# A conformer and sparse-attention decoder step: where the gate's loads land, and what the compressed branch and the cached rows queue behind

## The chip, the cores and the metric

The kernel runs on one core of one Trainium2 chip. The metric is the device time of one execution in microseconds (us); a comparison goes by the median of several executions. The core has five engines with an instruction queue each: PE (matrix products), DVE (vector), ACT (scalar activations and copies), POOL (a slower vector engine) and SP (which here only issues DMAs). A queue runs in order: an instruction that waits holds back all behind it on its engine.

## The reference

One inference step of a two-layer decoder, for a prompt of 512 tokens and 8 sequences of 4 new tokens each, 544 columns in all, width 1024. Only the first layer's first half and the cached keys matter here:

```
shift, scale, gate = split(silu(c) @ w_ada + b_ada)        # per sub-layer, width 3 x 1024
h = rmsnorm(x, g) * (1 + scale) + shift
u = h @ w_pw1 + b_pw1;  a, g = split(u);  u = a * sigmoid(g)
full = concat([state_conv, u])                             # 30 cached rows per decoded sequence
y = depthwise_conv(full, w_dw, 31 taps) + b_dw
x = x + gate * (silu(layernorm(y)) @ w_pw2 + b_pw2)
x = x + gate2 * swiglu(modulated rmsnorm(x))               # the first feed-forward layer
...
blk = cached pages, 32 rows a block, + pe_cmp              # compressed branch, of cached keys and values
cmp = silu(blk @ w_phi1 + b_phi1) @ w_phi2 + b_phi2        # used by the second layer's attention
```

The second layer is the attention (compressed, selected and window branches) and a second feed-forward layer.

## The kernel before

Activations stand with features on the 128 partitions: eight tiles f = 0 to 7 of 128 features, 544 columns each. A product in full precision is made of three products of split operands: each weight tile `raw` is split into `whi` (ACT, L169) and `wlo` (DVE, L170), the activations into `h_hi` and `h_lo`, and `products` (L176 to L186) issues, for each of eight k, three pairs of matmuls (L183, L185). So one product of 128 outputs is 48 matmuls, and each tile f of the convolution has two (gate and value).

**Order.** A scheduler puts each engine's instructions in an order ahead of time, by its own model of their durations, by program order and by priorities. `high_priority(-LATER)` marks a block as filler that goes into gaps. `issue_after(ins)` makes every instruction of its block that runs on the engine of `ins` stand behind `ins` in that engine's order; instructions of the block on other engines are bound only through their data.

**Buffers.** `raw` has four buffers of 512 KB. Every 512 KB load of weights goes into one of them, in the order of the program, and is issued on SP's queue, which stops until the buffer is free. `xt`, in the pool `shift`, has three buffers of just over two such slabs; the convolution uses them for shifted copies of its input (L714 to L724), the compressed branch for transposed cached rows.

**The stages that matter**, in order:

- *Modulation.* `ada_steps` (L446) makes one of scale, shift and gate: eight slabs of `w_ada`, each followed by four small matmuls (L452). `first_modulated` (L471) makes scale and shift of the first sub-layer; its generator `slabs` puts 12 of the 16 slabs two by two into `xt` and four into `raw`. The gate (`between` in `run`) uses `raw` alone, four slabs ahead of each tile f from f = 2 (`NSTEP`, L666).
- *Cached rows.* `state_parts` (L419) loads the cached convolution rows, transposes them on PE (16 transposes, L155), copies them on ACT (L431), multiplies them with the taps on POOL (16 multiplies, L439) and sums on DVE (16 reductions, L441). Its memory, the pool `setup`, then goes to the pool of the compressed branch.
- *Convolution.* `gated_units` (L645) makes `up` of each f (L677). Tiles 3 to 7 are convolved on PE as 64 matmuls of shifted copies (L730). Tiles 0 to 2 and half of tile 7 are convolved on DVE (`depthwise`, L734) as chains of 31 steps (L768), tile 7's chain last.
- *Layer norm and second product.* `layer_norm_out` (L798) sums over the features with PE (L812), subtracts the mean (L818), squares, takes the root and the reciprocal (L824), applies silu, splits, and multiplies with `w_pw2`; the residual follows.
- *Compressed branch.* `compress_steps` (L1032) takes the eight sequences one by one: two gathers of cached rows on POOL's DMA queue (`nat`, two buffers, L1030), four transposes on DVE (L1043), 32 matmuls of 128 columns on PE (L1049) and small work. For the first sequence it also makes a bias from `pe_cmp` (tile `hk`, DVE transpose L1025, 32 matmuls L1053, `bh` L1055). All 24 steps are issued as filler ahead of `depthwise`.
- *Feed-forward layer 0* follows, with what is left of the compressed branch, the bias tables, and the transposing and storing of all cached keys (`key_steps`, L1289) as its filler.

## Time and profile before

| what | value |
|---|---|
| time, median of 3 executions | 1660.17 us (1652.02 to 1661.15) |
| the profiled execution | 1661.26 us, span of its instructions 1659.5 us |
| PE busy | 1555.0 us, 94% of the span |
| DVE busy | 1107.8 us, 67% |
| ACT / POOL busy | 694.1 us, 42% / 235.2 us, 14% |
| moved by DMA | 295.26 MB, mean 178 GB/s |

A busy share is an average over stages that different engines limit. What a stage costs is read from the stretch of the profile where it lies: which engine is busy throughout, and which wait ends last. Times are counted from the span's start. In the profile each 32-bit matmul of these small products (L1049, L1053, L452, L812) shows as two passes, so its counts are double those of the program; the split products (L183, L185) show as one.

### The profile page before, as it was taken

The page shows a single profiled execution, that of the slowest core. Times are in us where ns is not written, and L with a number is a line of the kernel's source. Part 1 is how long each engine was busy: PE and PEld are TensorE (multiplying, and loading weights), DVE is VectorE, ACT ScalarE, POOL GpSimd, SP SyncE. Part 2 cuts the span into 40 slices and gives each one's busy share as a digit, 9 for nine tenths or more (in the row PEclk, how much of TensorE's full clock was granted, in tenths as well). Part 3 has the DMA queues.
Part 4 walks back from the last instruction along what each step waited for, and adds up shares of the span by engine and source line. Part 5 has one row for each costly group of instructions (what it writes and reads, how often), then busy time and mean ns, then how long its engine had stood idle before and what let it go on. Part 6 is the DMA issues. An engine that isn't in the chain of part 4 may idle for free.

```text
span 1659.5 us, 31626 instructions
## 1 busy us (share of the span) xinstructions
PE 1555.0 (94%) x12423; PEld 1366.8 (82%) x12423; DVE 1107.8 (67%) x2369; ACT 694.1 (42%) x1443; POOL 235.2 (14%) x270
## 2 busy tenths in 40 slices
PE   6897998999988889999999899999999999999997
PEld 3784677989978878999977677655699999999997
DVE  2897866482447788576657644867856865874865
ACT  5321115242222344255445422755746542552554
POOL 3444401021220112001110000000011110110010
PEclk9898979999999999999999999999999999999999
DMA  9577575374399999834779895746122472333231
GB/s 307 140 200 155 151 241 168 117 227 130 112 241 312 299 303 325 247 103 106 184 228 306 245 282 183 237 148 229 52 68 73 152 233 84 91 114 90 79 91 64
DMA packets 315568, 295.26 MB, mean 178 GB/s; under 512 B 16019, under 2 KB 275485, under 8 KB 311179
## 3 DMA queue, kind: packets, MB, share of 16 engines
q1 hardware_dynamic: 304507, 237.24, 48.7%
q0 software_dynamic: 10224, 55.47, 10.7%
q8 instruction: 98, 1.61, 0.4%
q10 hardware_dynamic: 688, 0.53, 0.1%
q14 instruction: 51, 0.42, 0.1%
HBM read 256.28 MB, written 45.48 MB: 182 GB/s over the span
## 4 chain that ended last, share of the span: by engine, by line
PE 65%; DMA 13%; DVE 10%; issue 6%; SPq 2%; ACT 2%; POOL 1%; ACTq 0%; DVEq 0%; POOLq 0%
PE g L185 18%; PE g L183 17%; PE g L247 8%; DMA raw<-in_w_down_dram 4%; PE t L247 3%; PE t L155 3%; PE o L1530 2%; DMA raw<-in_w_ada_dram 2%; DVE wlo L196 2%; PE t L1049 2%; PE a L452 1%; PE t L1379 1%; PE t L730 1%; PE sc L1509 1%; DVE y L768 1%
## 5 line engine op out<-in xcount | busy, mean ns | idle before, releaser
L169 ACT CAST whi<-raw 128x512 fp32r<-128x512 f32 x250 | 149.7, 606 | 408.7 <-PE g L185 280.1
L170 DVE TENSOR_TENSOR wlo<-raw,whi 128x512 fp32r<-128x512 f32 x250 | 173.0, 696 | 156.5 <-ACT whi L169 155.6
L183 PE MATMUL g<-h_hi,whi 128*128 128x256 f32 (+1 forms) x584 | 170.5, 293 | 13.9 <-DVE un L680 9.3
L185 PE MATMUL g<-h_hi,whi 128*128 128x288 f32 (+4 forms) x584 | 173.5, 298 | 0.9 <-ACT h_hi L575 0.9
L185 PE MATMUL g<-h_hi,wlo 128*128 128x288 f32 (+4 forms) x584 | 173.9, 298 | 0.0
L185 PE MATMUL g<-h_lo,whi 128*128 128x288 f32 (+4 forms) x584 | 173.7, 297 | 0.0
L183 PE MATMUL g<-h_lo,whi 128*128 128x256 f32 (+1 forms) x584 | 168.3, 288 | 3.0 <-DVE h_lo L830 3.0
L183 PE MATMUL g<-h_hi,wlo 128*128 128x256 f32 (+1 forms) x584 | 167.3, 287 | 0.0
L183 PEld LDWEIGHTS g<-h_hi,whi 128*128 128x128 f32 x584 | 111.5, 191 | 27.3 <-issue 16.2
L247 PE MATMUL g<-T,whi 128*128 128x272 f32 x656 | 127.9, 291 | 4.1 <-DVE sg L261 2.5
L195 ACT CAST whi<-s 128x512 fp32r<-128x512 f32 x128 | 79.1, 620 | 99.9 <-PE g L247 61.7
L183 PE MATMUL g<-a_hi,whi 128*128 128x256 f32 (+1 forms) x372 | 108.0, 291 | 12.4 <-ACT ht L912 4.3
L183 PEld LDWEIGHTS g<-h_lo,whi 128*128 128x128 f32 x584 | 111.8, 192 | 8.0 <-issue 4.3
L185 PEld LDWEIGHTS g<-h_hi,whi 128*128 128x128 f32 x584 | 111.3, 191 | 4.2 <-issue 2.9
L185 PEld LDWEIGHTS g<-h_hi,wlo 128*128 128x128 f32 x584 | 111.3, 191 | 2.6 <-issue 2.5
L185 PEld LDWEIGHTS g<-h_lo,whi 128*128 128x128 f32 x584 | 111.2, 190 | 2.6 <-issue 2.5
L183 PEld LDWEIGHTS g<-h_hi,wlo 128*128 128x128 f32 x584 | 111.5, 191 | 1.8 <-issue 1.7
L196 DVE TENSOR_TENSOR wlo<-s,whi 128x512 fp32r<-128x512 f32 x128 | 89.1, 698 | 34.0 <-ACT whi L195 32.2
L185 PE MATMUL g<-a_hi,wlo 128*128 128x288 f32 (+1 forms) x372 | 111.1, 299 | 0.0
L185 PE MATMUL g<-a_hi,whi 128*128 128x288 f32 (+1 forms) x372 | 110.9, 299 | 0.0
L185 PE MATMUL g<-a_lo,whi 128*128 128x288 f32 (+1 forms) x372 | 110.7, 298 | 0.0
L247 PEld LDWEIGHTS g<-T,whi 128*128 128x128 f32 x656 | 103.8, 190 | 5.6 <-ACT whi L195 2.2
(511 smaller groups left out, 4165.2 us busy)
## 6 DMA issues: line engine op xcount, KB each, us to landing
raw<-in_w_ada_dram SPq DMA_DIRECT2D x84, 512.0 KB
raw<-in_w_gate_dram SPq DMA_DIRECT2D x44, 512.0 KB
raw<-in_w_up_dram SPq DMA_DIRECT2D x44, 512.0 KB
raw<-in_w_down_dram SPq DMA_DIRECT2D x32, 512.0 KB
raw<-in_w_pw_dram SPq DMA_DIRECT2D x24, 512.0 KB
kt_d<-ktr SPq DMA_DIRECT2D x96, 128.0 KB
kt<-kt_d SPq DMA_DIRECT2D x24, 512.0 KB
raw<-in_w_kv_dram SPq DMA_DIRECT2D x20, 512.0 KB
```

The source lines that it names most:

```text
L155: self.te.transpose(out, in_, self.ident[:n, :n])
L169: self.s.copy(hi[:, :b - a], raw[:, a:b])
L170: self.v.tensor_tensor(out=lo[:, :b - a], in0=raw[:, a:b], in1=hi[:, :b - a].bitcast(F32), op=ALU.subtract)
L183: self.te.matmul(pg[:, 0, :split], a, b[:, i, :split], start=st, stop=sp)
L185: self.te.matmul(pg[:, 1, :tokens - split], a, b[:, i, split:tokens], start=st, stop=sp)
L195: self.s.copy(hi, src)
L196: self.v.tensor_tensor(out=lo, in0=src, in1=hi.bitcast(F32), op=ALU.subtract)
L247: self.te.matmul(out, a[:, i], b(i), start=first and i == 0 and j == 0, stop=i == 3 and j == 2, skip_group_check=not first)
L452: self.te.matmul(pa[32 * j:32 * j + 32, :256], self.cT[:, k, :], w[:, j * 256:(j + 1) * 256], start=k == 0, stop=k == KT - 1)
L730: self.te.matmul(pt[32 * gg:32 * gg + 32], wds[q // 4][:, gg, q % 4], vs[:, gg, 4 * q:4 * q + cols], start=q == 0, stop=q == 7)
L1049: te.matmul(ph[:, :P], self.w1[:, e, c // 2, c % 2], xv[:, c % 2, c // 2], start=c == 0, stop=c == 15)
L1530: te.matmul(po[rp * HD:(rp + 1) * HD, :256], self.vn[:, br, t, gg * HD:(gg + 1) * HD], pT[:, rp * 256:(rp + 1) * 256], start=br == 0 and t ...
```

## The change

Three edits. First, the generator of slabs becomes a method, `first_slabs`, that serves scale, shift and gate: 24 slabs, of which the last eight, the gate's, go into `xt` like most of those before, and none into `raw`. Second, the 24 steps of the compressed branch are issued after `depthwise` in the program, and inside `issue_after(self.last_step)`: their DVE instructions stand behind the last step of tile 7's chain. Third, the 16 transposes of the cached rows stand on PE behind the last matmul of the first tile's products (`first_product`).

```diff
--- before.py
+++ after.py
@@ -180,7 +180,7 @@
             whi, wlo = w[i]
             for j, (a, b) in enumerate([(whi, xhi), (whi, xlo), (wlo, xhi)]):
                 st, sp = i == 0 and j == 0, i == k - 1 and j == 2
-                self.te.matmul(pg[:, 0, :split], a, b[:, i, :split], start=st, stop=sp)
+                self.last_product = self.te.matmul(pg[:, 0, :split], a, b[:, i, :split], start=st, stop=sp).ins
                 if tokens > split:
                     self.te.matmul(pg[:, 1, :tokens - split], a, b[:, i, split:tokens], start=st, stop=sp)
         return pgs
@@ -427,7 +427,8 @@
             for f0 in range(0, KT, 4):
                 pt = self.bank()
                 for f in range(4):
-                    self.transpose(pt[:, f * 120:(f + 1) * 120], sc[:, a, (f0 + f) * P:(f0 + f + 1) * P])
+                    with self.tc.issue_after(self.first_product):
+                        self.transpose(pt[:, f * 120:(f + 1) * 120], sc[:, a, (f0 + f) * P:(f0 + f + 1) * P])
                 self.s.copy(us[:, f0:f0 + 4, a * 4:(a + 1) * 4, :CW - 1],
                             pt[:, :480].rearrange("p (f b w) -> p f b w", f=4, b=4))
         squares = sp.tile([P, D], F32, name="squares").rearrange("p (a n) -> p a n", a=2)[:, :, :4 * DS * (CW - 1)]
@@ -470,18 +471,7 @@
 
     def first_modulated(self, wsrc, rstd):
 
-        def slabs():
-            for i in range(2 * KT):
-                if 6 <= i < 10:
-                    yield self.wp.tile([P, KT, P], F32, name="raw", bufs=4).rearrange("p a b -> p (a b)")
-                else:
-
-                    if i % 2 == 0:
-                        two = self.shift_pool.tile([P, 4, SEQ + 28], F32, name="xt", bufs=3).rearrange("p a n -> p (a n)")
-                    yield two[:, i % 2 * D:(i % 2 + 1) * D]
-
-        made = slabs()
-        scale, shift = [self.ada_steps(0, part, b, lambda: next(made)) for part, b in ((1, "at"), (0, "bt"))]
+        scale, shift = [self.ada_steps(0, part, b, lambda: next(self.slabs)) for part, b in ((1, "at"), (0, "bt"))]
         for step in [scale] * KT + [shift] * 2:
             next(step)
         for _ in itertools.chain(scale, shift):
@@ -489,6 +479,17 @@
         ws = [self.weights(w) for w in wsrc]
         self.modulated(0, rstd)
         return ws
+
+    def first_slabs(self):
+
+        for i in range(3 * KT):
+            if 6 <= i < 10:
+                yield self.wp.tile([P, KT, P], F32, name="raw", bufs=4).rearrange("p a b -> p (a b)")
+            else:
+
+                if i % 2 == 0:
+                    two = self.shift_pool.tile([P, 4, SEQ + 28], F32, name="xt", bufs=3).rearrange("p a n -> p (a n)")
+                yield two[:, i % 2 * D:(i % 2 + 1) * D]
 
 
     def add_square(self, acc, src, f):
@@ -660,6 +661,7 @@
             cols = [wsrc[:, :, c * D + f * P:c * D + (f + 1) * P] for c in (1, 0)]
             if f == 0:
                 pg, pa = self.products(self.first_modulated(cols, self.rstd0), self.h_hi, self.h_lo, KT)
+                self.first_product = self.last_product
             else:
                 wg, wa = [self.weights(c) for c in cols]
                 for _ in range(NSTEP if f > 1 else 0):
@@ -765,8 +767,8 @@
                     if j == 0:
                         v.tensor_scalar(ps, x, w, self.b_dw[:, f:f + 1], op0=ALU.mult, op1=ALU.add)
                     else:
-                        v.scalar_tensor_tensor(out=ps, in0=x, scalar=w, in1=ps,
-                                               op0=ALU.mult, op1=ALU.add)
+                        self.last_step = v.scalar_tensor_tensor(out=ps, in0=x, scalar=w, in1=ps,
+                                               op0=ALU.mult, op1=ALU.add).ins
         for f in ORDER:
             finished(f, v)
         self.dump("y", y)
@@ -1674,7 +1676,8 @@
                 self.shift_pool = shifting.__enter__()
                 with sbuf("setup", "right") as sp:
                     self.setup(sp)
-                    between = self.ada_steps(0, 2)
+                    self.slabs = self.first_slabs()
+                    between = self.ada_steps(0, 2, slab=lambda: next(self.slabs))
                     ada1 = itertools.chain(*(self.ada_steps(1, part) for part in (1, 0, 2)))
                     units_ = self.gated_units(pool, between)
                     next(units_)
@@ -1684,13 +1687,13 @@
                 next(units_)
                 compress = self.compress_steps(self.compress_pool)
 
+                acc = self.depthwise(pool)
                 with tc.high_priority(-LATER):
                     for _ in between:
                         pass
-                    for _ in range(MID):
-                        next(compress)
-                acc = self.depthwise(pool)
-                with tc.high_priority(-LATER):
+                    with tc.issue_after(self.last_step):
+                        for _ in range(MID):
+                            next(compress)
                     self.conv_states(pool)
                 self.layer_norm_out(pool, acc, ada1)
             self.dump("x1", self.x)
```

What this does to the order shows at three places. SP's queue, from the last loads of the shift to the loads of the compressed branch's first weights (in_w_phi, 16 of 128 KB) and of `hk` (in_pe_cmp); in_w_ada are the modulation's slabs, in_w_pw the convolution's weights. Before:

```order
L450 DMA xt<-in_w_ada_dram 128x1024 x6
L163 DMA raw<-in_w_pw_dram 128x8x128 x2
L423 DMA xt<-in_state_conv_dram 120x2x1024
L163 DMA raw<-in_w_pw_dram 128x8x128 x4
L450 DMA raw<-in_w_ada_dram 128x1024 x4
L163 DMA raw<-in_w_pw_dram 128x8x128 x2
L450 DMA raw<-in_w_ada_dram 128x1024 x4
L163 DMA raw<-in_w_pw_dram 128x8x128 x3
L1004 DMA w_1798<-in_w_phi_dram 32x8x128 x4
L163 DMA raw<-in_w_pw_dram 128x8x128
L1004 DMA w_1798<-in_w_phi_dram 32x8x128 x9
L163 DMA raw<-in_w_pw_dram 128x8x128
```

And with the change:

```order
L451 DMA xt<-in_w_ada_dram 128x1024 x6
L163 DMA raw<-in_w_pw_dram 128x8x128 x2
L423 DMA xt<-in_state_conv_dram 120x2x1024
L163 DMA raw<-in_w_pw_dram 128x8x128 x2
L451 DMA xt<-in_w_ada_dram 128x1024 x6
L163 DMA raw<-in_w_pw_dram 128x8x128 x4
L451 DMA xt<-in_w_ada_dram 128x1024 x2
L163 DMA raw<-in_w_pw_dram 128x8x128 x7
L1006 DMA w_1958<-in_w_phi_dram 32x8x128 x10
L163 DMA raw<-in_w_pw_dram 128x8x128
L1006 DMA w_1958<-in_w_phi_dram 32x8x128 x6
```

The gate's eight slabs go into `xt`, six of them ahead of tile 2's weights; the branch's weights come behind 15 of the 16 loads of w_pw1, where before they came behind 11. The loads of `hk` move far down, behind the stores of the convolution's states.

DVE's queue, around the chain of tile 7 (L768 to L770 write `y` from `up`; L1043 and L1045 are the branch's transposes). Before:

```order
L766 TENSOR_SCALAR y<-up,vec 128x256
L1043 STREAM_TRANSPOSE xt<-nat 128x1024 x2
L745 TENSOR_TENSOR acc<-acc,y 128x544
L768 SCALAR_TENSOR_TENSOR y<-up,vec,y 128x256 x3
...
L1055 TENSOR_SCALAR bh<-t,vec 128x1
L768 SCALAR_TENSOR_TENSOR y<-up,vec,y 128x256 x3
L1043 STREAM_TRANSPOSE xt<-nat 128x1024 x2
L1064 TENSOR_SCALAR cks<-t,b2k 64x64 x2
L768 SCALAR_TENSOR_TENSOR y<-up,vec,y 128x256 x4
L745 TENSOR_TENSOR acc<-acc,y 128x544
```

And with the change:

```order
L770 SCALAR_TENSOR_TENSOR y<-up,vec,y 128x256 x18
L1021 MEMSET hk 128x64
L1045 STREAM_TRANSPOSE xt<-nat 128x1024 x4
L806 TENSOR_TENSOR ts<-mod,vec 128x8x9
L747 TENSOR_TENSOR acc<-acc,y 128x544
...
L1027 STREAM_TRANSPOSE peT<-hk 128x64
L1045 STREAM_TRANSPOSE xt<-nat 128x1024 x2
L820 SCALAR_TENSOR_TENSOR y<-g,y 128x544 x8
```

Eight transposes and `bh` leave the chain; four transposes stand between the chain and the last addition to `acc`, and two more, with the transpose of `hk`, ahead of the mean's subtraction (L820).

PE's queue, from the first products of the convolution, which begin behind the last transposes of `ada_sb`. Before, and then with the change:

```order
L155 MATMUL t<-c_small,ada_sb 128x128 x2
L183 MATMUL g<-h_hi,whi 128x256
L185 MATMUL g<-h_hi,whi 128x288
L183 MATMUL g<-h_lo,whi 128x256
L183 MATMUL g<-h_hi,whi 128x256
L185 MATMUL g<-h_hi,whi 128x288
L183 MATMUL g<-h_lo,whi 128x256
L155 MATMUL t<-c_small,xt 128x120 x8
```

```order
L183 MATMUL g<-h_lo,whi 128x256
L185 MATMUL g<-h_lo,whi 128x288
L183 MATMUL g<-h_hi,wlo 128x256
L185 MATMUL g<-h_hi,wlo 128x288
L155 MATMUL t<-c_small,xt 128x120 x8
L453 MATMUL a<-xt,cT 32x256 x8
L183 MATMUL g<-h_hi,whi 128x256
L185 MATMUL g<-h_hi,whi 128x288
```

The first eight transposes of the cached rows stood behind six matmuls of tile 0; now they stand behind all 96 of them, with two slabs of the gate, and the other eight behind tile 1's. Counted over the whole order of PE, 113 of the branch's 256 matmuls stood ahead of the end of the second product before, and 43 do now; its last one stands 127 split matmuls further into the feed-forward layer.

## Rows read from the trace of the kernel before

**Rows 1.** page, part 1: busy us (share of the span) xinstructions
```profile
PE 1555.0 (94%) x12423; PEld 1366.8 (82%) x12423; DVE 1107.8 (67%) x2369; ACT 694.1 (42%) x1443; POOL 235.2 (14%) x270
```

**Rows 2.** busy time by window: columns us, engines busy (x), PEclk, DMA share, GB/s
```profile
61.00:126.00 65.00, 57.49 (x463) 53.22 (x462) 64.60 (x84) 15.33 (x30) 33.80 (x22) 0.95 0.64 174
126.00:140.00 14.00, 5.09 (x41) 4.79 (x39) 3.44 (x8) 2.00 (x4) 2.42 (x6) 0.85 0.95 198
140.00:197.00 57.00, 56.29 (x448) 37.92 (x452) 49.92 (x80) 9.81 (x17) 29.69 (x35) 0.95 0.53 129
197.00:234.00 37.00, 31.96 (x270) 21.41 (x259) 28.52 (x53) 3.62 (x8) 10.41 (x16) 0.78 0.78 256
234.00:286.00 52.00, 46.59 (x352) 39.69 (x352) 35.70 (x57) 28.49 (x49) 5.64 (x7) 0.96 0.53 176
365.00:438.00 73.00, 73.00 (x604) 71.92 (x603) 27.93 (x46) 18.43 (x33) 8.44 (x9) 1.00 0.37 110
460.00:690.00 230.00, 206.72 (x1580) 193.24 (x1579) 162.98 (x274) 77.73 (x149) 31.91 (x28) 0.96 0.99 302
```

**Rows 3.** waits of PE, 0 to 360 us: total us, times, longest
```profile
PE a L452 <- DMA raw<-in_w_ada_dram: 10.7, 5, 4.9
PE g L183 <- DVE un L680: 9.3, 1, 9.3
```

**Rows 4.** waits of DVE, 60 to 900 us: total us, times, longest
```profile
DVE peT L1025 <- DMA raw<-in_w_pw_dram: 10.6, 1, 10.6
DVE bh L1055 <- PE t L1053: 7.6, 1, 7.6
DVE xt L1043 <- DMA nat<-in_cache_kv_cmp_dram,rows: 2.8, 4, 1.3
```

**Rows 5.** timeline of DVE: start us, busy us, instruction, count, wait
```profile
61.36 0.75 DVE L677 SCALAR_TENSOR_TENSOR upv<-g,vec,ht 128x512 f32<-128x512 f32 x1 [1.31 <-ACT ht L675]
63.36 1.91 DVE L768 SCALAR_TENSOR_TENSOR y<-upv,vec,y 128x512 f32<-128x512 f32 x1
145.93 4.72 DVE L768 SCALAR_TENSOR_TENSOR y<-upv,vec,y 128x512 f32<-128x512 f32 x7
197.16 0.73 DVE L677 SCALAR_TENSOR_TENSOR up<-g,vec,ht 128x512 f32<-128x512 f32 x1
234.04 0.72 DVE L745 TENSOR_TENSOR acc<-acc,y 128x544 f32<-128x544 f32 x1
240.56 1.99 DVE L818 SCALAR_TENSOR_TENSOR y<-g,y 128x544 f32<-128x544 f32 x3 [2.35 <-PE g L812]
```

**Rows 6.** timeline of PE, two places
```profile
45.94 1.83 PE L155 MATMUL t<-c_small,xt 120*128 120x120 f32 x8 [1.69 <-DMA xt<-in_state_conv_dram]
335.72 0.94 PE L1049 MATMUL t<-xt,w 128*128 128x128 f32 x6
```

**Rows 7.** timeline of POOL, two places
```profile
62.90 7.77 POOL L439 TENSOR_TENSOR squares<-xt,vec 128x480 f32<-128x480 f32 x4
147.85 10.43 POOL L710 TENSOR_TENSOR wd<-c_small,w 128x512 f32<-128x512 f32 x2 [1.57 <-PE t L730]
```

**Rows 8.** DVE by line, 197 to 234 us: count, busy us, mean ns, idle
```profile
L768 DVE SCALAR_TENSOR_TENSOR y<-up,vec,y 128x256 f32<-128x256 f32 x30 | 14.9, 496 | 0.8
L1043 DVE STREAM_TRANSPOSE xt<-nat 128x1024 f32<-128x1024 f32 x8 | 9.6, 1223 | 0.0
```

**Rows 9.** the gathers into nat, 25 to 240 us
```profile
L1030 POOL DMA_INDIRECT nat<-in_cache_kv_cmp_dram,rows x6: 944/1002/1358, 104.8 to 231.7; - x6
DMA to landing us min/median/max: 5.6/8.0/10.6
```

**Rows 10.** PE by line, 240 to 336 us, then 335.7 to 440 us
```profile
L1049 PE MATMUL t<-xt,w 128*128 128x128 f32 x156 | 21.2, 289 | 0.0
L1049 PE MATMUL t<-xt,w 128*128 128x128 f32 x294 | 37.7, 276 | 0.0
```

**Rows 11.** DMA, 460 to 690 us
```profile
DMA packets 77764, 69.35 MB, mean 302 GB/s; under 512 B 3320, under 2 KB 73238, under 8 KB 75697
```

## The prediction

> **What bounds the kernel.** I read the page's busy shares first, then busy time by stage, then the waits of PE and DVE, then single places of the timelines. PE is busy 94% of the span [rows 1], so what can be won is PE's idle time, PE's work at a low clock, and work that moves under other work. By stage [rows 2] PE is full in feed-forward layer 0 (365 to 438), and has gaps in 61 to 126 us (7.5 us), 126 to 140 (8.9), 197 to 234 (5.0) and 234 to 286 (5.4). From 460 to 690 the DMA engines are 0.99 busy and PE waits 23.3 us. In 61 to 126 DVE is fuller than PE: 64.6 of 65.0.
>
> The waits name the gaps: PE waits 10.7 us in five times for slabs of the gate, and once 9.3 us for `un` of DVE [rows 3]. DVE makes `un` late because it stands 10.6 us at `peT`, the transpose of `hk` [rows 4]. The trace names a load of `raw` there; what had long to come are the loads of `hk`, issued behind the branch's weights. The same list shows 7.6 us at `bh`, which waits for 64 passes of PE and lies in the middle of tile 7's chain.
>
> The marks of the stage are on DVE's timeline [rows 5]: `upv` of tile 0 at 61.4, `up` of tile 7 at 197.2, the last addition behind tile 7's chain at 234.0, the mean's subtraction at 240.6. The second product ends at about 335.7, where PE takes up a run of the branch's matmuls [rows 6].
>
> **The change part by part.** I sum against the profiled execution, 1661.3 us with its surroundings, 1.1 above the median. A measurement of this kernel can tell about 0.5%, 8.3 us, from no change.
>
> *Transposes of the cached rows behind tile 0's products.* Before, eight of them stood inside the first product: PE waited 1.69 us for the load and spent 1.83 on them [rows 6]. They leave the first product and come behind it, where their load has landed. That start can come earlier by 0 (if the load of the product's weights is next) to 3.5 us. I take **−2**, the middle: the weights of the product come in the same queue as that load, and some of the wait may fall on them instead. POOL's multiplies do not start later for it: the first ran at 62.9, behind `ut` of tile 0 [rows 7].
>
> *Gate slabs into `xt`, and the branch off DVE's way up to tile 7.* From 61.4 to 197.2 is 135.8 us. DVE loses the wait at `peT`, 10.6 [rows 4]. PE loses part of the 10.7 us for slabs; 7.5 us of idle time lie in 61 to 126, where DVE is full, and the slabs no longer hold buffers that tile 2's and 3's weights need. So PE's gain counts only where DVE stood behind PE: I take 4 us, half of the 7.5. That is **−14.6**. [...]
> What speaks against more is the sharing between DVE and POOL. A chain step of 512 columns takes 1.91 us where POOL multiplies four squares in 7.77 [rows 5, 7], and 4.72 / 7 = 0.67 where POOL does not run one, and POOL's pair of `wd` takes 10.43 beside such steps [rows 7]. Sixteen multiplies run in both kernels, so I let them cost the same. [...] I go by the rows, where the multiplies lay beside a full DVE already.
>
> *Chain of tile 7.* Eight transposes [rows 8] leave it, 9.2 us net of overlap; so does `bh`'s wait, 7.6, and two small steps, 0.5. **−17.3**: the chain is then its 30 steps and little else, 14.9 us of the 37 [rows 8]. What would be late next is PE's tile 6, which only has its 64 passes to do behind the last product; they fit.
>
> *From the chain's end to the subtraction.* Before, 6.5 us, of which most is PE's sums of tile 7 [rows 5]. Now DVE has four transposes there (they lie beside the sums), then `peT`, then two transposes of the third gather. That gather can be issued only when the first buffer of `nat` is free: two transposes 2.4, issue 1.0, landing 8.0, its own two transposes 2.4 [rows 8, 9], which is 13.8; less 0.2 for overlap, 13.6. DVE runs in order, so the subtraction waits for a transfer that it does not need: **+7.1**. By the landing of 5.6 or 10.6 [rows 9] it is +4.7 to +9.7.
>
> *From the subtraction to the end of the second product.* Before, 95.2 us (240.6 to 335.7). In it PE made 156 passes of the branch, 21.2 us, 0.136 each [rows 10]; by the new order 54 are left, so 102 × 0.136 = 13.9 go; five of nine transposes go from DVE, 5.8 us, and waits on gathers, up to 2.8 [rows 4]. PE is not full from 234 to 286, so not all of 13.9 + 8 counts: **−14**, bounds −8 (the passes lay half in gaps) to −20.
>
> These five make −40.8: the second product ends at about 295.
>
> *The branch's rest, now under feed-forward layer 0.* PE is busy 73.0 of 73.0 there [rows 2], so nothing is hidden: by the order 226 passes of the branch stood ahead of the second product's end and 86 do now, so 140 more come behind it, at 37.7 / 294 = 0.128 [rows 10] are 18.0, at the rate of the split matmuls' stage, 0.121, 16.9: **+17**. So of the gain 13.9 is a move and not a gain.
>
> *The loads from 460 on.* The cached keys' filler comes behind the branch's. Its last matmul stands 127 split matmuls later, 127 × 0.131 = 16.6 us (206.7 / 1580 in the last of [rows 2]) into the layer. The loads of weights run on meanwhile: those of 127 / 48 = 2.6 products, 1.4 MB, at 302 GB/s [rows 11] 4.6 us. A stage that the DMA engines fill (0.99) ends later by up to 12.2, counted from the layer's start; PE's 23 us of waiting there can take some of it, or not. **+8**, between 0 and 12.2, nearer to the upper end because the DMA engines are full.
>
> Sum: −2 − 14.6 − 17.3 + 7.1 − 14 + 17 + 8 = −15.8; 1661.3 − 15.8 = **1645**.
>
> **The rivals.**
> *PE bounds the front and the loads' shift is hidden.* −23.5 in place of −14.6 and 0 in place of +8: −32.7, about 1629. For it: PE is at 0.99 of 140 to 197 already, and PE has 23 us of slack from 460 to 690. Against it: DVE is full from 61 to 126. Chance 0.20. With −20 at the second product it is about 1623, the low end.
> *The gain is eaten.* Every term at its upper bound: 0 − 12.6 − 17.3 + 9.7 − 8 + 18 + 12.2 = +2: 1663, no change that can be told. For it: the moved passes come back in full, in a stage without a gap. Chance 0.15.
> *POOL's multiplies hold DVE.* They start behind tile 0's and 1's products now, and if eight more of the 16 meet chain steps, each costs DVE 1.91 − 0.67 = 1.24 us [rows 5], 9.9 in a stretch where DVE is full: 1655, no change that can be told. For it: the rows of the pair; against it: before, too, they ran beside a full DVE. Chance 0.05. [...]
> *Slower: gathers hold DVE under feed-forward 0.* Ten of the 16 gathers are left behind the second product; before it was six. Their transposes stand in DVE's order between the `wlo` halves, and PE stops when those run out. From issue to landing a gather takes 9.0 us [rows 9], and its successor's transposes stand some 10 us behind. If each of the ten holds DVE so long that PE loses 2.7 us, that is +27, 1672. It decides when landing goes past some 10 us in the layer, whose weights come at the same time. Against it: DVE waited for `nat` only 2.8 us in four times before [rows 4], and DVE is 0.38 busy there [rows 2]. Chance 0.12.
> [...] Chance 0.06.
> *The change does not do what it says*, as where DVE still waits for something of the branch's first weights ahead of tile 7: 1661. The order speaks against it. Chance 0.02.
>
> **How the numbers follow.** The forecast has 0.40. Faster by over 0.5% are the forecast and the first rival, 0.60; within 0.5% the eaten gain, POOL, the clock and the last, 0.28; slower the gathers, 0.12. The range goes from 1623, the first rival's lower end, to 1664, above the eaten gain; the gathers are left out, and a little at the low end.
>
> **What would show it.** Right: no wait of PE for gate slabs and none of 9.3 us for `un`; `up` of tile 7 near 180.5; a chain of some 17 us without a transpose of `nat`; the subtraction 13 to 14 us behind the chain's end, after a DVE wait for `nat`; the second product's end near 295; the branch's last matmul near 429 where it was at 438; and PE's waits from 460 to 690 a few us above 23. Wrong: `up` of tile 7 later than 190 (then DVE and POOL, not the waits, set the front), the second product's end later than 315, waits of PE behind DVE's gathers in the first feed-forward layer, or a granted clock under 0.9 in the second product.

## The result, and the profile after

The changed kernel takes 1670.07 us (median of 11 executions, 1662.51 to 1676.12) against 1660.17 us: ratio 1.0056, 95% interval 1.0034 to 1.0079. It is slower by a little more than 0.5%, where 1645 was forecast. The profiled execution took 1666.48 us, span 1664.7 (before: 1661.26 and 1659.5).

Busy time by stage after, in the columns of [rows 2]:

```profile
61.00:126.00 65.00, 57.06 (x443) 54.85 (x442) 64.75 (x78) 14.39 (x27) 33.73 (x27) 0.92 0.31 88
126.00:140.00 14.00, 14.00 (x120) 8.83 (x119) 14.00 (x22) 2.68 (x5) 4.62 (x6) 1.00 1.08 302
197.00:234.00 37.00, 29.59 (x225) 18.54 (x226) 22.22 (x42) 10.36 (x23) 3.60 (x4) 0.75 0.71 231
234.00:286.00 52.00, 49.18 (x351) 44.65 (x350) 31.45 (x53) 26.73 (x40) 1.53 (x2) 0.88 0.35 117
```

The DMA engines do half as much in 61 to 126 now (0.31, before 0.64): the slabs have come early. But DVE is as full as it was (64.75 of 65), and PE's idle time there is 7.9 us where it was 7.5. The waits of PE, 0 to 360 us, in the columns of [rows 3], show what took the slabs' place (the change's line numbers are one or two higher than before's):

```profile
PE g L183 <- DVE un L682: 7.9, 2, 4.7
...
PE a L453 <- DMA raw<-in_w_ada_dram: 6.0, 3, 2.9
PE t L732 <- DMA xt<-up_d: 3.7, 1, 3.7
```

Two waits for slabs (4.9 and 2.6 us) became two for `un` (3.2 and 4.7), and the wait of 9.3 us behind `peT` became one of 3.7 for the shifted copies of `up`. The chain and what follows it, on DVE's timeline (columns of [rows 5]):

```profile
187.96 0.73 DVE L679 SCALAR_TENSOR_TENSOR up<-g,vec,ht 128x512 f32<-128x512 f32 x1
...
198.54 9.33 DVE L770 SCALAR_TENSOR_TENSOR y<-up,vec,y 128x256 f32<-128x256 f32 x18
207.84 0.11 DVE L1021 MEMSET hk<- 128x64 f32 x1
207.87 4.56 DVE L1045 STREAM_TRANSPOSE xt<-nat 128x1024 f32<-128x1024 f32 x4
...
227.54 0.25 DVE L1027 STREAM_TRANSPOSE peT<-hk 128x64 f32<-128x64 f32 x1 [10.67 <-DMA hk<-in_pe_cmp_dram]
...
230.63 5.10 DVE L820 SCALAR_TENSOR_TENSOR y<-g,y 128x544 f32<-128x544 f32 x8
```

`up` of tile 7 comes 9.2 us earlier than before, the chain is as short as forecast, and then DVE stands 10.7 us at `peT`, for the loads of `hk`. The zeroing that they need was done by 207.95. But in SP's queue they stand behind stores of the convolution's states, and SP itself waited 6.0 us ahead of the first of them. SP's timeline, and the line of its waits, 185 to 235 us:

```profile
212.70 2.09 SPq L796 DMA_DIRECT2D out_dram<-wd  x5
220.89 0.28 SPq L1025 DMA_DIRECT2D hk<-in_pe_cmp_dram  x1
221.27 0.36 SPq L451 DMA_DIRECT2D raw<-in_w_ada_dram  x1
222.23 2.30 SPq L1025 DMA_DIRECT2D hk<-in_pe_cmp_dram  x7
```

```profile
SPq L1025 <- DMA raw<-in_w_pw_dram: 6.0, 1, 6.0
```

The subtraction also needs PE's sums over the features, and these were hardly earlier than `hk`: PE's order has filler and steps of the next modulation ahead of them, and PE waited 2.9 us for a slab of these. PE's timeline:

```profile
222.26 0.94 PE L453 MATMUL a<-raw,cT 128*32 128x256 f32 x8 [2.90 <-DMA raw<-in_w_ada_dram]
...
227.08 1.08 PE L814 MATMUL g<-acc,ones 128*128 128x272 f32 x4
```

Both traces have 5736 split matmuls (L183 and L185), so their ends, counted through on PE's timeline, compare stage by stage. The column on the left gives the count at which a stage ends; the table is worked out from the timelines, us:

| stage, up to split matmul | before ends | after ends | gained (−) or lost so far | by the stage |
|---|---|---|---|---|
| convolution's products, 768 | 195.6 | 186.4 | −9.2 | −9.2 |
| second product, 1152 | 334.2 | 312.4 | −21.8 | −12.6 |
| feed-forward 0 to the branch's end, 1728 | 453.8 | 446.5 | −7.3 | +14.4 |
| to the attention's projections, 3200 | 851.0 | 847.2 | −3.8 | +3.5 |
| attention's projections, 3744 | 994.6 | 999.5 | +4.9 | +8.6 |
| the rest, 5736 | 1636.7 | 1641.7 | +5.0 | +0.1 |

So the front does gain, less than forecast; most of it is given back in feed-forward 0; and 8.6 us are lost in a stage that no edit touches. The +3.5 of the loads' stage (1728 to 3200) says little: that stage took 385 to 405 us over the 20 profiles of this document (397.2 before, 400.7 with the change).

In the stage of the attention's projections the order of the attention's small work among the projections had changed too: the scheduler moved the last score products and softmax steps some 20 to 30 split matmuls forward, and the last products with values some 29 back. PE's waits from 840 to 1010 us, before and then after:

```profile
PE b L1443 <- DVE os_lo L1461: 4.1, 1, 4.1
```

```profile
PE g L155 <- DVE ht L1208: 6.7, 1, 6.7
PE b L1445 <- DMA vs<-in_cache_kv_win_dram: 2.3, 1, 2.3
```

And the stretch from 900 to 1000 us, before and then after (columns of [rows 2]): PE idles 10.0 us in place of 6.9, and its clock is 0.93 in place of 0.98, which on 90 busy us is another 4.5.

```profile
900.00:1000.00 100.00, 93.10 (x955) 73.81 (x954) 57.08 (x195) 39.98 (x98) 2.89 (x4) 0.98 0.91 265
```

```profile
900.00:1000.00 100.00, 90.02 (x901) 71.19 (x899) 51.32 (x178) 36.64 (x85) 3.14 (x4) 0.93 0.85 248
```

### The profile page after: what moved, and what is told of

Its sections match the earlier page's. It is cut to its first block, busy times and chain, and to the rows that moved or that the text cites. A ratio compares the mean times of both kernels' runs of the same rounds, so it can differ in the third digit from the quotient of the medians.

```text
span 1664.7 us, 31621 instructions
## 1 busy us (share of the span) xinstructions
PE 1562.4 (94%) x12423; PEld 1372.3 (82%) x12423; DVE 1109.1 (67%) x2369; ACT 696.1 (42%) x1443; POOL 230.5 (14%) x270
## 4 chain that ended last, share of the span: by engine, by line
PE 65%; DMA 15%; DVE 12%; issue 4%; ACT 2%; SPq 1%; POOL 0%; ACTq 0%; DVEq 0%; POOLq 0%
PE g L185 16%; PE g L183 15%; PE g L247 10%; PE t L247 3%; DMA raw<-in_w_ada_dram 3%; PE t L155 3%; PE t L1051 3%; DMA raw<-in_w_gate_dram 2%; PE o L1532 2%; DVE wlo L196 2%; DVE y L770 2%; DMA raw<-in_w_down_dram 1%; PE a L453 1%; PE t L1381 1%; DVE wlo L170 1%
## 5 line engine op out<-in xcount | busy, mean ns | idle before, releaser
L183 PE MATMUL g<-h_hi,whi 128*128 128x256 f32 (+1 forms) x584 | 172.7, 297 | 12.8 <-DVE un L682 7.9
L185 PE MATMUL g<-h_lo,whi 128*128 128x288 f32 (+4 forms) x584 | 175.3, 300 | 0.6 <-DVE h_lo L577 0.6
L185 PE MATMUL g<-h_hi,whi 128*128 128x288 f32 (+4 forms) x584 | 174.9, 300 | 0.9 <-ACT h_hi L576 0.9
L185 PE MATMUL g<-h_hi,wlo 128*128 128x288 f32 (+4 forms) x584 | 174.5, 299 | 0.0
L183 PE MATMUL g<-h_lo,whi 128*128 128x256 f32 (+1 forms) x584 | 168.8, 289 | 0.4 <-DVE h_lo L562 0.4
L183 PE MATMUL g<-h_hi,wlo 128*128 128x256 f32 (+1 forms) x584 | 168.9, 289 | 0.0
L183 PEld LDWEIGHTS g<-h_hi,whi 128*128 128x128 f32 x584 | 113.1, 194 | 28.9 <-issue 17.0
L183 PEld LDWEIGHTS g<-h_hi,wlo 128*128 128x128 f32 x584 | 113.0, 193 | 4.3 <-issue 4.2
L185 PEld LDWEIGHTS g<-h_hi,whi 128*128 128x128 f32 x584 | 113.1, 194 | 3.3 <-issue 2.1
L183 PEld LDWEIGHTS g<-h_lo,whi 128*128 128x128 f32 x584 | 113.1, 194 | 3.1 <-issue 2.4
L185 PEld LDWEIGHTS g<-h_lo,whi 128*128 128x128 f32 x584 | 112.4, 192 | 3.3 <-issue 2.3
L183 PE MATMUL g<-a_hi,whi 128*128 128x256 f32 (+1 forms) x372 | 107.1, 288 | 7.7 <-DVE x L641 3.1
L185 PEld LDWEIGHTS g<-h_hi,wlo 128*128 128x128 f32 x584 | 112.6, 193 | 1.2 <-issue 1.2
L185 PE MATMUL g<-a_hi,wlo 128*128 128x288 f32 (+1 forms) x372 | 110.5, 297 | 0.0
L185 PE MATMUL g<-a_hi,whi 128*128 128x288 f32 (+1 forms) x372 | 110.2, 297 | 0.0
L183 PE MATMUL g<-a_lo,whi 128*128 128x256 f32 (+1 forms) x372 | 105.2, 283 | 5.0 <-POOL a_lo L922 5.0
L185 PE MATMUL g<-a_lo,whi 128*128 128x288 f32 (+1 forms) x372 | 109.8, 296 | 0.0
```

What stands on the lines that cost most here:

```text
L183: self.last_product = self.te.matmul(pg[:, 0, :split], a, b[:, i, :split], start=st, stop=sp).ins
L185: self.te.matmul(pg[:, 1, :tokens - split], a, b[:, i, split:tokens], start=st, stop=sp)
```

## The experiments

All were timed against the kernel before on the same chip; a ratio is to it. How far one profiled execution can be read, a version that was run twice (below) shows: its split matmul 1728 ended at 441.7 and at 449.7 us, its attention stage (split matmuls 3200 to 3744; 143.7 us before, 152.3 with the change) took 145.2 and 146.0. Differences of under some 8 us at that point are therefore not read from single profiles, those of the attention stage are. The expectations have the attention stage some 1 us shorter, at 143 and 151.

**Two suspects: hk and the attention's order.** First `hk` early, with only `peT` behind the chain:

```diff
         self.compress_loads(pool)
+        yield
+        self.v.transpose(self.peT, self.pe.rearrange("p (h i) -> p h i", h=2))
...
+                    next(compress)
                     with tc.issue_after(self.last_step):
```

> The change, with the zeroing and the loads of hk taken out of the block that stands behind tile 7's chain; only its transpose peT stays there. Order of PE in the attention stage as in the change. Theory F (the front: the subtraction waits 10.7 us for hk, whose loads start only behind the chain): the subtraction comes some 14 us behind the chain's end in place of 22.8, the second product ends 5 to 9 us earlier than in the change, and the whole is 3 to 8 us shorter than the change, ratio to before about 1.001 to 1.004. Theory L (a ledger of PE: its work up to the branch's last matmul is the same, and it idled only a few us while DVE waited for hk): the marks move, but behind the branch's last matmul at most 3 us are left; ratio 1.004 to 1.006. Theory O (the attention's order costs 8 to 9 us): the stretch between split matmuls 3200 and 3744 takes about 151 us as in the change, against 143 before.

Second, the same with that `next(compress)` ahead of `depthwise`:

> As the run before it, but with the branch's loads issued in the program ahead of depthwise, by which the scheduler gives the attention the same order on PE as before the change. Theory O: the stretch between split matmuls 3200 and 3744 takes about 143 us, as before the change, and the whole is 8 to 9 us shorter than the run with hk early alone: ratio to before 0.995 to 0.999. Against O (the stretch is longer because its transfers come at other times): about 151 us again, ratio as in the run with hk early alone.

Third, the change without `with self.tc.issue_after(self.first_product):`

> The change without its third edit: the transposes of the cached rows stand inside tile 0's products again. By the scheduler's choice the attention has before's order on PE. Theory O: the stretch between split matmuls 3200 and 3744 takes about 143 us, and the whole is 6 to 9 us shorter than the change: ratio to before 0.998 to 1.001, though hk is still late and the first product is 2 us longer. Theory F alone: ratio about 1.006 to 1.007, 2 us longer than the change.

Fourth, the change with the branch ahead of `depthwise` again and no `issue_after(self.last_step)`:

> The change without its second edit: the branch is issued ahead of depthwise again and its transposes lie in tile 7's chain; slabs in xt and late transposes of the cached rows stay. Attention in before's order. Theory F: DVE waits for hk ahead of tile 7 again, up of tile 7 comes near 195, but no moved passes in feed-forward 0; ratio 0.996 to 1.000. Theory L: the two stalls of PE on slabs, 7.5 us, are gone and are the only thing that PE's ledger gains: 1652 to 1656, ratio 0.995 to 0.998.

Measured: 1.0058 (1.0034 to 1.0082), 0.9988 (0.9960 to 1.0017), 1.0002 (0.9978 to 1.0025), 0.9997 (0.9973 to 1.0022). Attention stage: 154.2, 145.3, 145.4, 143.7 us. `hk` early gained nothing, so F is wrong: the wait at `peT` went, and the subtraction waited for PE's sums instead. It came 20.2 us behind the chain's end, where the change has 22.8 and F had some 14. DVE's waits from 60 to 300 us in the first of these runs show it, and PE's timeline there has a slab ahead of the sums again:

```profile
DVE y L820 <- PE g L814: 7.7, 1, 7.7
```

```profile
228.82 1.08 PE L453 MATMUL a<-raw,cT 128*32 128x256 f32 x8 [4.65 <-DMA raw<-in_w_ada_dram]
...
231.71 2.02 PE L814 MATMUL g<-acc,ones 128*128 128x272 f32 x4
```

The three with before's order in the attention are level with before; O stands. The first two differ only in whether the branch's loads and the gate's last steps are issued behind `depthwise` or ahead of it, and their medians by 7.1 us (1669.57 and 1662.48). L misses in the fourth: it had 0.995 to 0.998 for the slab waits gone, but PE waited 8.0 us for `un` there.

**The attention's order by itself.** `LATER = 1000` is the filler's priority; a small change of it leaves the front's order nearly alone but flips the scheduler between the two orders of the attention. The change with 998, then the kernel before with 850 and with 880:

> The change whole, with the priority of the filler lowered by 998 in place of 1000. The order of PE in the front stays the change's but for single places; in the attention stage alone (split matmuls 3200 to 3744) the scheduler falls back to before's order. Theory O (that order is what costs): the stretch takes 143 to 145 us in place of 151, and the whole is 7 to 9 us shorter than the change, ratio to before 0.998 to 1.001. Theory T (the stretch is longer because transfers or the clock fall differently behind the new front): 151 us still, ratio 1.004 to 1.008.

> The kernel before, with none of the three edits, and the filler's priority lowered by 850 in place of 1000: the scheduler gives the attention stage the order that it has with the change; the front differs a little from before. Theory O: the stretch of split matmuls 3200 to 3744 takes 151 to 153 us in place of 143, and the whole is 7 to 10 us longer than before, ratio 1.004 to 1.007, without any part of the change. Theory T: 143 us, ratio 0.998 to 1.002.

> The control to the run before it: the kernel before with 880, by which the front differs from before about as much, and the attention stage keeps before's order. Theory O: 143 us in the stretch, ratio 0.998 to 1.002. If the shifted front and not the attention's order makes the difference, it is as long as the run with 850.

Measured: 0.9978 (0.9951 to 1.0006), 1.0025 (1.0005 to 1.0044), 1.0045 (1.0026 to 1.0064); attention stage 145.1, 153.4 and 146.4 us. The stage answers as O has it: by the traces PE's order in it is before's in the first of these runs, matmul for matmul, and the change's in the second. The whole does so only for the change (1.0056 to 0.9978, 13 us; 7.2 of them in this stage). With 850 and 880 O misses the whole, for which it had 1.004 to 1.007 and 0.998 to 1.002. The run with 880 is no good control, because what comes ahead moved too: split matmul 3200 ends at 845.0 us with 850 and at 855.3 with 880 (before: 851.0). So the totals of these two neither bear O out nor speak against it. Over all 20 profiles the stage took 142.4 to 146.4 us in the 16 with the old order or one near it, and 151.1 to 154.2 in the 4 with the new one. In the 16 PE waits 3.7 to 6.8 us for `os_lo` in this stage; in the four it waits 6.7 to 8.6 for `ht` and 2.3 to 3.6 for a load. Here from before with 850:

```profile
PE g L155 <- DVE ht L1206: 8.6, 1, 8.6
```

**What binds the front.** The change without the multiplies and reductions of the cached rows; before with hk's loads moved ahead of w1's; and both moves without the second edit:

```diff
-                self.g.tensor_tensor(out=pr, in0=win, in1=...)
-                self.v.tensor_reduce(out=self.ys0[:, f, ...], ...)
+                if b0 == 0 and f == 0:
+                    self.v.memset(self.ys0[:, :, :], 0.0)
```

> The change without the cached rows' 16 multiplies on POOL and 16 reductions on DVE (their sum is set to zero, so that part of the convolution is left out); order of PE in the attention as in the change. Theory D (DVE, with POOL's multiplies beside it, is what the front waits for once the slabs are in time): DVE is relieved of 16 x 0.64 us and of up to 16 x 1.24 us beside the multiplies, 10 to 30 us; PE's two waits for un, 7.9 us, are gone, up of tile 7 comes at 176 to 182 in place of 188, and from the start to the branch's last matmul 8 to 12 us go: ratio to before 0.998 to 1.001, where the change had 1.0056. Theory P (PE's work and other waits bind): the waits for un go, others of PE take their place, at most 3 us go, ratio 1.003 to 1.006.

> The kernel before with one move and no part of the change: the zeroing and the loads of hk are issued ahead of the branch's first weights in place of behind them; PE's order is before's throughout. If DVE's wait of 10.6 us at peT and PE's of 9.3 us behind it cost their length: both are gone, and the kernel is 7 to 9 us shorter, ratio 0.994 to 0.997. If another wait stands behind them (POOL's wd, the shifted copies of up, PE's own work): 0 to 3 us, ratio 0.998 to 1.001.

> The first and third edits of the change without the second, and hk's loads ahead of the branch's weights; attention in before's order. If the waits for slabs (7.5 us) and for peT (10.6) add up: ratio 0.990 to 0.994. If DVE's full stretch takes back what the slabs give (PE waited 7.9 us for un in the change) and only the wait at peT counts: ratio 0.994 to 0.998. If neither counts: 0.998 to 1.001.

Measured: 0.9951 (0.9928 to 0.9973), 1.0011 (0.9988 to 1.0035), 0.9976 (0.9956 to 0.9995). Without the cached rows' work no wait for `un` is left, `up` of tile 7 comes at 173.8 us, and split matmul 1728 ends at 432.3 against 446.5, somewhat more than D expected, though the attention has the slow order (151.1). So theory D holds. PE is full in the stretch (columns of [rows 2]):

```profile
61.00:126.00 65.00, 65.00 (x548) 57.92 (x545) 62.52 (x98) 16.54 (x31) 13.78 (x23) 1.00 0.76 199
```

The same shows tile by tile. Split matmul 288 ends tile 2's products and 480 tile 4's; ends in us, over the 20 profiles:

| cached rows' work | kernels | 288 ends | 480 ends |
|---|---|---|---|
| in place, slabs early and transposes late | the change and 5 runs | 85.8 to 87.5 | 124.7 to 126.6 |
| in place, not both of these edits | before and 6 runs | 91.5 to 97.1 | 124.8 to 128.6 |
| left out, or behind tile 4 (below) | 3 runs | 86.7 to 88.3 | 113.3 to 114.9 |
| spread (below) | 4 runs | 86.5 to 95.5 | 122.4 to 123.5 |

A lead of some 8 us from early slabs and late transposes is gone two tiles later, unless DVE and POOL are relieved.

In the second run DVE's wait at `peT` was down to 0.7 us, and nothing came of it: PE's 9.3 us for `un` became 5.0 for the shifted copies, and the other waits stayed:

```profile
PE a L452 <- DMA raw<-in_w_ada_dram: 12.5, 5, 5.0
...
PE t L730 <- DMA xt<-up_d: 5.0, 1, 5.0
```

In the third DVE still waited 10.2 us at `peT`, since the scheduler had put hk's loads between those of w1. So it tells little of the sum of both.

**Late sums.** If the cached rows' work is in the way, it can be put later. The reductions behind `un` of tile 4 (with hk early; then without the second edit). In the program the multiplies and reductions then stand behind the whole convolution, in a method of their own, so the branch's memory also comes free later; the diff shows the line that sets the place:

```diff
+                with self.tc.issue_after(self.uns[4]):
                     self.v.tensor_reduce(out=self.ys0[:, f, ...], ...)
```

> The change with hk's loads early (as in the first run), and with the 16 reductions of the cached rows on DVE put behind un of tile 4 (POOL's multiplies follow them, since they have two buffers); attention in before's order. Theory D: the stretch up to tile 4 is free of DVE's and POOL's work on the cached rows, PE's two waits for un (7.9 us) go as they did without that work; the work comes back beside tiles 5 to 7, where DVE had 7 us free. Front to the branch's last matmul 3 to 10 us shorter than the change; with the attention's 8 us the whole is 11 to 18 us shorter than the change, ratio 0.994 to 0.999. Theory D wrong (the order in which DVE does the same work is all one): as the second run, 0.998 to 1.001.

> The same late reductions on the change without its second edit (the branch lies in tile 7's chain again); attention in before's order. Theory D: PE's waits for un go here too, ratio 0.992 to 0.997, below the 0.9997 of the run without the second edit. If DVE's wait for hk ahead of tile 7 takes the gain: 0.997 to 1.001.

Measured: 1.0092 (1.0063 to 1.0121) and 1.0027 (1.0007 to 1.0046), a miss. Up to tile 4 all came as hoped (its `up` at 115.4 us, 129.0 in the change). Then PE waits for copies of `up`, 6.6 us and 7.2 us. The first ones POOL issued only at 153.9 us, with multiplies in its queue ahead of them. The next ones took some 12 us from issue to landing, beside gathers and the branch's first weights, which come late here. PE's waits for slabs have grown as well, to 14.7 us from 6.0; why, no run shows. Waits of PE in the first of the two runs, and POOL busy 38.6 of 57 us:

```profile
PE a L459 <- DMA raw<-in_w_ada_dram: 14.7, 5, 7.1
PE t L738 <- DMA xt<-up_d: 7.6, 2, 6.6
PE g L738 <- DMA xt<-up_d: 7.2, 1, 7.2
```

```profile
140.00:197.00 57.00, 43.14 (x337) 29.65 (x333) 50.85 (x78) 7.88 (x14) 38.61 (x47) 0.88 0.65 156
```

**Spread sums, and edits alone.** The same line with `self.uns[f * 2 // 3]`: on the change (with 998), and on the version with slabs, late transposes and hk first, without the second edit. Then the first and the second edit by themselves:

> The whole change (hk late), with the reductions of the cached rows spread: four behind un of tile 0, two behind tile 1's, four behind tile 2's, two behind tile 3's, four behind tile 4's; filler's priority 998, so that the attention has before's order. If the place of the work is what counts: PE's two waits for un shrink from 7.9 us to under 4, POOL's copies are not held up as when all came behind tile 4, front 3 to 6 us shorter than in the run of the change with the old attention (ratio 0.9978): 0.994 to 0.997. If its amount counts: the waits move to later tiles, 0.997 to 1.001.

> The same spread on the run with slabs, late transposes and hk's loads first, without the second edit (ratio 0.9976 there); attention in before's order. Place counts: 0.993 to 0.996. Amount counts: 0.997 to 1.001.

> The first edit alone (gate slabs in xt); attention in before's order. If PE's waits for slabs were worth their length: 7 us shorter, ratio 0.995 to 0.997. If DVE takes them back as waits for un: 0.998 to 1.001, with two waits of PE for un of 6 to 9 us together in the front.

> The second edit alone (branch behind tile 7's chain); attention in before's order. By the ledger of PE: the waits for slabs stay (7.5 us), the wait of 9.3 us for un goes or shrinks; from the first product to the branch's last matmul 0 to 6 us less than before, ratio 0.996 to 1.001. If the moved passes and the late hk cost more than the waits: ratio 1.002 to 1.006.

Measured: 0.9960 (0.9941 to 0.9979), 0.9919 (0.9893 to 0.9945), 0.9980 (0.9951 to 1.0008), 0.9986 (0.9960 to 1.0012). The first and second edits alone are no change that can be told (no run has the third by itself); with the slabs alone PE waits for `un` 2.3 and 3.8 us, as expected if DVE takes them back. On the change the spread cannot be told from none (0.9960, without it 0.9978). Without the second edit it beats both kernels, at 1646.4 us, the median of 4 executions; there DVE's wait at `peT` had gone down to 1.9 us as well. PE's waits in it:

```profile
PE a L459 <- DMA raw<-in_w_ada_dram: 4.2, 5, 1.4
PE g L183 <- DVE un L688: 3.3, 2, 1.8
PE g L738 <- DMA xt<-up: 3.1, 1, 3.1
...
PE g L183 <- DVE wlo L170: 2.8, 2, 2.3
```

Last, the spread and hk first on the kernel before, with no edit of the change, and the best version again:

> The kernel before with the spread sums and hk's loads first, and none of the three edits. If the slabs gain only where DVE is relieved (theory D), PE waits 7 to 8 us for slabs here that it does not wait with them: ratio 0.995 to 0.998, some 5 us above the version with slabs and late transposes. If the spread alone does it: 0.990 to 0.994.

> The version with slabs, late transposes, hk first and spread sums once more: ratio 0.990 to 0.995, front to the branch's last matmul some 401 us as before, against 413 of the kernel before.

Measured: 0.9938 (0.9908 to 0.9968) and 0.9937 (0.9911 to 0.9963). The first of these differs from before with hk first (1.0011) by the spread alone. So with hk first the spread does it, and slabs and transposes add nothing that can be told; the expectation that slabs gain once DVE is relieved is not borne out, though one slab wait of 4.3 us is still there without them. How much of the spread's gain lies on DVE and how much on POOL no run parts.

## Why the prediction was wrong

Its terms, beside what the two profiles show (the first two parts together end at `up` of tile 7):

| step | forecast | measured | from |
|---|---|---|---|
| first product, up to tile 7's `up` | −16.6 | −9.2 | 197.16 to 187.96 |
| tile 7's chain | −17.3 | −17.0 | 36.9 to 19.9, `up` to chain's end |
| chain's end to subtraction | +7.1 | +16.2 | 6.5 to 22.8 |
| subtraction to second product's end | −14 | −11.8 | 93.6 to 81.8 |
| branch's rest in feed-forward 0 | +17 | +14.4 | the table above |
| loads behind it | +8 | +3.5 | the table above |
| attention's order | none | +8.6 | the table above |

In these two profiles the steps of the chain, of the moved passes and of the second product came within 3 us of the forecast. Three failed.

*Up to tile 7.* The prediction counted half of PE's waits for slabs and all of DVE's wait at `peT` as won. In their place it let nothing come but POOL's multiplies, at a chance of 0.05. It had the row that speaks against it: DVE full in 61 to 126 [rows 2]. The slabs won nothing there. At split matmul 288 the change was 9.3 us ahead (85.8 against 95.1), at 480 it was 0.2 (124.7 against 124.9): DVE was busy all of the 38.9 us between, PE waited 7.9 us for `un`, and its clock was 0.87, in before's stretch 1.00. The wait at `peT` did come in: at 576, behind tile 5's products, the change was 12.6 ahead (144.0 against 156.6). Then 3.4 were lost again by 768; PE waits 3.7 us for the shifted copies in between. What set the stretch was DVE with POOL beside it: leaving out their work on the cached rows gave `up` of tile 7 14.2 us earlier. Of DVE's busy time up to split matmul 768 that took 24.9 us (133.8 to 108.9). The 16 reductions are 10.2 of them; and of 121 steps and `wlo` halves of 512 columns 21 took over 1 us with the change, and 4 without that work, which by their excess over 0.74 us is an estimate of 18. The two do not add up exactly, and no run has one without the other. Before there were 19 such long ones: so where the rival of POOL's multiplies had eight more and 9.9 us, two more came, some 3 us by the same estimate. With the change 13 of the 21 took 1.92 to 2.05 us, each beside one of the multiplies.

Of the bounds that the rivals take for this step, −12.6 is the 10.6 at `peT` and 2 of the 4. In −23.5 are all of PE's idle time in the first three windows of [rows 2], 17.1, and an estimate of 6.4 for their clock at 1.00, which no run shows: with the change 13.5 us of idle time were left in these windows, and the clock was 0.92, 1.00 and 1.00.

*From the chain's end to the subtraction.* The prediction took the third gather for the transfer that comes last, and PE's sums as done beside the transposes. It was `hk` that came last on DVE, whose loads the edit had moved far down SP's queue; the order showed it. The sums were hardly earlier: PE made them at 227.1 to 228.2 us, behind filler and a slab. So `hk` by itself cost next to nothing: with hk early the subtraction still came 20.2 us behind the chain's end, waiting for PE.

*The attention.* This is what made the sign: with before's order there the same edits, whole or in part, came out at 0.9978 to 1.0002. The sum ends at the loads and takes the rest as unmoved; it looked for reordering only where the diff has its edits. An order computed ahead of time for the whole program is one thing: a shift early in it flipped a choice some 700 us later. No rival had it.

The slower rival (gathers holding DVE under feed-forward 0) was not it: that stage lost 14.4 us, less than forecast. The clock, a rival at a chance of 0.06, was lower in part: 0.88 in 234 to 286 where it was 0.96, an estimate of some 4 us on 49 busy us; no run shows what lowered it there. In 197 to 234 it was 0.75, and PE waited three times, 2.2 to 2.9 us each, for transfers. Before, it was 0.85 in 126 to 140 with a wait of 9.3 us for DVE and none for a transfer. What sets the clock no run shows.

One bound of the sum was off by 0.2: 16.6 − 4.6 is 12.0, not 12.2, for the loads.

One check would have warned: up to the branch's last matmul PE does the same work in both kernels. Its waits of over 0.25 us between 40 and 340 us sum to 34.2 us before and 28.4 after. A net gain of 23.8 at that point, as forecast (−40.8 + 17), would have needed two thirds of them to go with nothing in their place, or a higher clock, and that stayed at 0.92 and 0.91.

Of the difference in the medians, 9.9 us, the profiles show 5.2. The rest lies within what executions of one kernel differ by (before 1652 to 1666), and no run took it apart.

## What to carry to other kernels

Before counting the waits of an engine as won, ask which other engine is full in that stretch: here the waits for slabs that went there, 4.9 and 2.6 us, came back as 3.2 and 4.7 for DVE, and the gain came from relieving DVE and POOL there, by spreading side work over more tiles (ratio 0.992 to 0.994 in three runs), not from bringing data earlier. Where a scheduler orders the whole program, compare its order in every stage, not only around the edits, and run a version that differs in that alone, such as a filler's priority changed by 2 in 1000 (changes of 120 and 150 moved other stages too), before a part of the time is laid to the edit. And keep a ledger of the busiest engine: work that only moves is no gain, and the waits that it had, with what it ran at a granted clock below 1.00, are the most that can be won.

## What the runs showed that was not expected

- A wait could be removed, whole or nearly, with no effect on the time that could be told, three times: 7.5 us for slabs, 10.6 at `peT` (down to 0.7 us, ratio 1.0011), and 10.7 for `hk`.
- The stage of the attention's projections took 142.4 to 146.4 us or 151.1 to 154.2, and nothing between, by its order alone, whatever the front was.
- One and the same kernel, profiled twice, differed by 8 us at split matmul 1728 and by 1 in the attention stage: in this pair the front, with its waits for transfers, is where the two executions differ.
